# A hybrid decoder block on one core: score products issued in pairs on two row halves of TensorE, SSD products alternating between two column halves

## The chip, the core and the metric

The kernel runs on one core of a Trainium2 chip. Times are microseconds (us) of device time of one execution. The engines are TensorE (PE, with its weight loads listed as PEld), VectorE (DVE), ScalarE (ACT), GpSimd (POOL) and SyncE (SP), which issues most transfers. Each works through its own instructions in order.

## The reference, cut to what matters

One block over 1024 tokens of width 1024. Differential attention and a Mamba-2 SSD mixer read the same modulated input, are merged by gates, and a PEER layer follows that retrieves 128 experts a token. Two parts matter here.

```python
scores = jnp.einsum('bqhjd,bkhjd->bhjqk', q[:, q0:kend], k[:, :kend]).astype(jnp.float32) * scale
p = jax.nn.softmax(scores + bias[None, :, None], axis=-1)
a = p[:, :, 0] - lam * p[:, :, 1]
...
w = cb[..., None] * decay_ts * dtc[:, None]
y = jnp.einsum('btsgr,bsgrp->btgrp', w, xc)
y = y + jnp.einsum('btgn,bgrpn->btgrp', cc, state) * jnp.exp(cum)[..., None]
```

Each of the 8 attention heads has two score matrices (j = 0, 1), both with a contraction over 64 channels. Each of the 32 SSD heads gives 64 channels of y. Everything is in float32.

## The kernel before, in words

The tokens are worked in two halves of 512. A half goes through projections, attention, the SSD mixer, the merge, the first norm and the PEER scores; then the program does the same for the second half, and a dense PEER stage follows that goes through all experts for some token tiles. For the other tiles the experts' rows are gathered by indirect transfers on POOL ("side" work), and the top-16 routing on DVE is "urgent" work. A Python planner (`drive`, `step`) lays side and urgent steps between the steps of the main generator by costs written in the program (the numbers that are yielded). The order inside an engine is then set by the framework's scheduler, which follows priorities and its own simulated times. So an edit at one place can move instructions at others.

Most of TensorE's work is `projs` (L269): products of 128 rows by 128 columns with 512 moving columns, each split in three for precision. They have one record each in the trace. A float32 product (scores, SSD, transposes) has two records, so a count of 384 at L436 means 192 products.

Scores (`att_scores`, L420 to 457). A unit is one head and one tile of 128 queries; it has nk tiles of keys, 1 to 4 in the first half of the tokens and 5 to 8 in the second. `att_scores(u, j)` issues the products of one j: channels 64j to 64j+63, so they use one half of TensorE's rows (L436), in pieces of at most 512 keys, each into a PSUM bank of the tag "S", of which there are 3. DVE adds the bias, takes the minimum and frees the bank (L440). ScalarE takes the exponential (L445), and behind the second j DVE combines the two (L452 to 458). `attention` calls it for j = 0, lays in some projection work, and calls it for j = 1.

SSD (`ssd_head`, `ssd_pair`). `ssd_head` prepares a head's operands: it loads the running sums (`cr`), ScalarE makes the decays `w` and exponentials (L738 to 743), DVE multiplies them (L747, L752), and it returns a list `mm` of products: 5 a head in the first half (three of 256 columns, two of 128), 6 in the second (four and two). `ssd_pair` (L758) runs the lists of two heads into one bank: the first head's output takes partitions 0 to 63 and so uses columns 0 to 63 of TensorE, the second's the other 64 columns. All of the first list is issued, then all of the second. `ssd` calls it four times for each of four groups in each half of the tokens, 32 pairs in all, and prepares the next two heads behind each pair.

Of the kernel before, what the change touches and what calls it, by code (L numbers as in the profile page):

```python
# [11 lines left out]
F32 = mybir.dt.float32  # L12
# [4 lines left out]
AF = mybir.ActivationFunctionType  # L17
ALU = mybir.AluOpType
AX = mybir.AxisListType

P = 128
# [26 lines left out]
class Block:  # L48
# [370 lines left out]
        hd.ms = self.mp.tile([P, 4], F32, name="att_m", tag="att_m", bufs=2)  # L419
        return hd  # L420

    def att_scores(self, u, j):

        nc, hd = self.nc, u.hd
        n = u.nk * P
        off = 896 - (u.nk - 1) * P
        if j == 0:
            u.e, u.st = [], self.mp.tile([P, 10], F32, name="att_s", tag="att_s", bufs=6)
        e, st = self.four(f"e{j}"), u.st
        r = slice(j * 64, j * 64 + 64)  # L430

        low = 3.0e38
        for c0 in range(0, n, 512):
            w = min(512, n - c0)
            sc = self.psum("ps_s", tag="S")
            nc.tensor.matmul(  # L436
                sc[:, :w], hd.q[r, u.qt * P : u.qt * P + P], hd.ks[c0 // 512][r, :w], start=True, stop=True
            )
            at = 8 + j if c0 + w < n else j
            nc.vector.tensor_tensor_reduce(  # L440
                e[:, c0 : c0 + w], sc[:, :w], hd.bias[:, off + c0 : off + c0 + w], scale=-0.125,
                scalar=low, op0=ALU.add, op1=ALU.min, accum_out=st[:, at : at + 1],
            )
            low = st[:, at : at + 1]
        nc.scalar.activation(  # L445
            e[:, :n], e[:, :n], AF.Exp, scale=-1.0, bias=st[:, j : j + 1],
            accum_out=st[:, 2 + j : 3 + j],
        )
        u.e.append(e)
        if j:  # L450

            nc.vector.reciprocal(st[:, 4:6], st[:, 2:4])  # L452
            nc.vector.tensor_scalar(
                st[:, 6:7], st[:, 2:3], st[:, 5:6], self.neg_lam, op0=ALU.mult, op1=ALU.mult
            )
            nc.vector.scalar_tensor_tensor(
                u.e[0][:, :n], e[:, :n], st[:, 6:7], u.e[0][:, :n], op0=ALU.mult, op1=ALU.add
            )

    def att_turn(self, u):  # L460
# [38 lines left out]
    def attention(self, hb, hT, heads, big, start):  # L499

        fill, prev, done = iter(()), None, None

        def more(n=1):
            for x in islice(fill, n):
                yield x

        t = 0.43 + 0.4 * hb
        for i in range(4 * HEADS + 1):
            h, qt = divmod(i, 4)
            u = None  # L510
            if h < HEADS:
                if qt == 0:
                    while len(heads) <= h:
                        yield from more()
                    hd = self.head(hb, h, big[h], heads[h])
                u = SimpleNamespace(hd=hd, qt=qt, nk=hb * 4 + qt + 1)
            if u:
                self.att_scores(u, 0)
                yield t
            if qt != 0:  # L520
                yield from more()
            if u:
                self.att_scores(u, 1)
                yield t
            if prev:
                self.att_turn(prev)
                yield t
            if qt != 2:
                yield from more()
            if prev:  # L530
                self.att_values(prev)
                yield t
                if prev.qt == 3:
                    done = prev.hd
                    self.att_norm(done)
                elif prev.qt == 1 and done:
                    self.att_out(done)
            yield from more(99 if qt == 0 else 1)
            if qt == 0 and h + 1 == HEADS:
                fill = self.ssd_start(hb, hT, start)  # L540
            elif qt == 0 and h + 1 == len(heads):
                fill = self.qkv(hb, h + 1, hT, heads)
            prev = u
        self.last_head = done
# [213 lines left out]
    def ssd_pair(self, heads):  # L758

        yp = self.psum("ps_y", tag="S")  # L760
        for half, mm in enumerate(heads):
            for i, (o, n, l, r) in enumerate(mm):
                self.nc.tensor.matmul(  # L763
                    yp[half * 64 : half * 64 + 64, o : o + n], l, r, start=i == 0, stop=i == len(mm) - 1,
                    skip_group_check=True,
                )
        return yp
# [771 lines left out]
```

## Time and profile before

| | |
|---|---|
| time, median of 3 runs | 4873.54 us (4871.61 to 4889.75) |
| the profiled execution: its time | 4892.37 us |
| its span in the trace | 4890.7 us |
| TensorE busy | 4064.6 us (83%) |
| DVE busy | 2973.5 us (61%) |
| POOL busy | 1853.8 us (38%) |

The first half's SSD stage lies at about 440 to 920 us, the second half's attention at 1110 to 1500, its SSD stage at 1500 to 2230; the dense stage begins near 2670. A busy share is an average over the span; what bounds a stage is read from that stage. The start of a matmul's record is measured; its end is modelled, and the records of neighbours overlap, so the time that a product takes is read here from start to start.

### The profile page before, as it was taken

To read this page: it belongs to the slowest core of one execution; us is meant where nothing else is said; L and a number is where in the kernel's file an instruction comes from. 1 tells how busy PE (TensorE), PEld (TensorE's weight loads), DVE (VectorE), ACT (ScalarE), POOL (GpSimd) and SP (SyncE) were. 2 spreads that over 40 slices of the span, in tenths; PEclk is the share of its full clock that TensorE was granted. 3 is DMA by queue.
4 is the path that set the end of the run, shared out by engine and by line. 5 is a ranking of instruction groups with operands and counts; after the bars stand their busy time and mean duration, and the time that the engine had idled before them with its cause. 6 is when DMAs were issued, how large, how long until landed. Compare 5 with 4: busy or idle time off the path is not lost.

```text
span 4890.7 us, 52580 instructions
## 1 busy us (share of the span) xinstructions
PE 4064.6 (83%) x17996; PEld 2780.7 (57%) x17996; DVE 2973.5 (61%) x6965; ACT 1424.4 (29%) x2340; POOL 1853.8 (38%) x1720
## 2 busy tenths in 40 slices
PE   6999898998988999998765856867999888998155
PEld 4777676776656755556652425756656775556000
DVE  7664545558999853458973147999322884226920
ACT  3544444323343442432211112322222222222000
POOL 1000000000225743345385546454343674334774
PEclk7999999999898999999876975988999999999588
DMA  7323232443555866678688852998888998888998
GB/s 274 107 76 114 71 106 93 130 150 100 168 165 175 288 218 223 216 264 299 196 276 278 311 212 86 304 307 302 283 284 281 351 353 293 276 287 319 363 359 317
DMA packets 443648, 1134.14 MB, mean 232 GB/s; under 512 B 141852, under 2 KB 164532, under 8 KB 443380
## 3 DMA queue, kind: packets, MB, share of 16 engines
q0 software_dynamic: 191008, 676.42, 39.8%
q1 hardware_dynamic: 218804, 405.04, 25.5%
q10 hardware_dynamic: 33568, 49.32, 2.8%
q8 instruction: 143, 2.34, 0.2%
q14 instruction: 125, 1.02, 0.1%
HBM read 1066.51 MB, written 63.06 MB: 231 GB/s over the span
## 4 chain that ended last, share of the span: by engine, by line
PE 38%; DVE 15%; issue 12%; DMA 10%; POOL 7%; ACT 2%; SPq 1%; ACTq 0%; POOLq 0%; DVEq 0%
PE ps_y L1285 7%; PE ps_u L269 7%; PE ps_v L1325 6%; POOL grow L1177 5%; DVE grow L1120 4%; DMA grow<-in_peer_u,ei 3%; DMA grow<-in_peer_v,ej 3%; PE ps_x L269 3%; POOL second_k L1254 3%; PE ps_b L269 2%; DVE wlo L220 2%; PE ps_z L269 2%; PE ps_pq L269 2%; PE ps_y L763 2%; PE ps_g L269 2%
## 5 line engine op out<-in xcount | busy, mean ns | idle before, releaser
L1177 POOL DMA_INDIRECT grow<-in_peer_u,ei x640 | 848.1, 1325 | 970.1 <-DVE grow L1120 312.6
L1177 POOL DMA_INDIRECT grow<-in_peer_v,ej x640 | 669.5, 1046 | 804.9 <-PE ps_y L1285 668.6
L220 DVE TENSOR_TENSOR wlo<-wraw,whi 128x1024 fp32r<-128x1024 f32 x498 | 607.3, 1221 | 522.8 <-ACT whi L219 414.5
L219 ACT CAST whi<-wraw 128x1024 fp32r<-128x1024 f32 x498 | 519.9, 1047 | 1379.5 <-PE ps_u L269 523.7
L1120 DVE SCALAR_TENSOR_TENSOR grow<-grow,gh 128x1024 f32<-128x1024 f32 x640 | 771.6, 1221 | 93.9 <-DMA grow<-in_peer_u,ei 89.3
L1285 PE MATMUL ps_y<-grow,own 128*32 128x512 f32 x2560 | 609.9, 629 | 105.9 <-DMA grow<-in_peer_v,ej 76.8
L269 PE MATMUL ps_u<-hhi,whi 128*128 128x384 f32 x1024 | 363.9, 355 | 53.3 <-ACT whi L219 45.6
L269 PE MATMUL ps_u<-hhi,wlo 128*128 128x384 f32 x1024 | 364.2, 356 | 38.7 <-DVE wlo L220 38.7
L1254 POOL TENSOR_SCALAR second_k<-iota_c,at 128x128 f32<-128x128 f32 x384 | 301.1, 794 | 236.5 <-PE ps_gate L1285 183.8
L1147 DVE COPY own<-wt 128x4 f32<-128x4 f32 x160 | 29.7, 189 | 563.3 <-PE ps_y L1285 506.1
L978 POOL DMA_DIRECT2D h2s_d<-bighi x8 | 4.5, 561 | 936.3 <-ACT bighi L245 936.1
L269 PE MATMUL ps_u<-hlo,whi 128*128 128x384 f32 x1024 | 355.1, 347 | 0.0
L1285 PEld LDWEIGHTS ps_y<-grow,own 128*32 128x32 f32 x2560 | 90.1, 111 | 423.2 <-DMA grow<-in_peer_v,ej 205.1
L1285 PE MATMUL ps_gate<-first_k,second_k 128*128 128x128 f32 x768 | 195.7, 396 | 122.0 <-POOL second_k L1254 87.5
L1325 PE MATMUL ps_v<-wlo,ehi 128*128 128x512 f32 x768 | 257.2, 409 | 27.3 <-DVE wlo L220 27.0
L1325 PE MATMUL ps_v<-whi,ehi 128*128 128x512 f32 x768 | 226.6, 408 | 58.4 <-ACT whi L219 40.0
L269 PEld LDWEIGHTS ps_u<-hhi,whi 128*128 128x128 f32 x1024 | 201.2, 196 | 117.8 <-ACT whi L219 56.1
L269 PEld LDWEIGHTS ps_u<-hhi,wlo 128*128 128x128 f32 x1024 | 200.2, 196 | 98.2 <-DVE wlo L220 63.5
L1285 PEld LDWEIGHTS ps_gate<-first_k,second_k 128*128 128x128 f32 x768 | 155.5, 257 | 169.6 <-POOL second_k L1254 126.5
L1325 PE MATMUL ps_v<-whi,elo 128*128 128x512 f32 x768 | 251.2, 403 | 0.0
L1325 PEld LDWEIGHTS ps_v<-whi,ehi 128*128 128x128 f32 x768 | 142.4, 192 | 119.5 <-ACT whi L219 47.6
L269 PEld LDWEIGHTS ps_u<-hlo,whi 128*128 128x128 f32 x1024 | 200.7, 196 | 14.6 <-issue 10.9
(342 smaller groups left out, 8098.9 us busy)
## 6 DMA issues: line engine op xcount, KB each, us to landing
wraw<-in_w_in SPq DMA_DIRECT2D x160, 512.0 KB
wraw<-in_peer_uT SPq DMA_DIRECT2D x128, 512.0 KB
wraw<-in_peer_v SPq DMA_DIRECT2D x128, 512.0 KB
wada<-in_w_adaT SPq DMA_DIRECT2D x48, 512.0 KB
g_d<-gs ACTq DMA_DIRECT2D x48, 512.0 KB
gl<-g_d SPq DMA_DIRECT2D x48, 512.0 KB
cr<-cum_d SPq DMA_DIRECT2D x64, 256.0 KB
wraw<-in_w_ssd SPq DMA_DIRECT2D x32, 512.0 KB
```

Of the source, the lines that this page charges most:

```text
L219: nc.scalar.copy(hi, raw)
L220: i = nc.vector.tensor_tensor(lo, raw, hi.bitcast(F32), op=ALU.subtract)
L269: i = self.nc.tensor.matmul(ps, w[x][:, k, :], r[y][:, k, :], start=k + n == 0, stop=k == kk - 1 and n == 2)
L763: self.nc.tensor.matmul(yp[half * 64 : half * 64 + 64, o : o + n], l, r, start=i == 0, stop=i == len(mm) - 1, skip_group_check=True,)
L978: nc.gpsimd.dma_start(self.h2s_d[part][:, k, :], big[k][part][:, g0:])
L1120: nc.vector.scalar_tensor_tensor(u, u, 1.0, h2, op0=ALU.mult, op1=ALU.mult, accum_out=act[:, k : k + 1])
L1147: nc.vector.tensor_copy(own[:, :, OWN - 1].rearrange("p (h r) -> p h r", h=2), wt[:, b * n : b * n + n].rearrange("p (h r) -> p h r", h=2) ...
L1177: self.nc.gpsimd.indirect_dma_start(out=r, out_offset=None, in_=table, in_offset=bass.IndirectOffsetOnAxis(ap=ei[:, k : k + 1], axis=0),)
L1254: nc.gpsimd.tensor_scalar(second, self.iota_c, at[:, 1, k : k + 1], None, op0=ALU.is_equal)
L1285: return op(*args, **kw)
L1325: nc.tensor.matmul(acc[2 * tt + c], prev[x][:, tt * P : tt * P + P], v[y].rearrange("p k c -> p (k c)")[:, c * 512 : c * 512 + 512], start ...
```

## The change

`att_scores` is called once for each piece of 512 keys instead of once for each j. It takes two banks, issues the two products of the piece next to each other (row halves 0 and 1), then the two DVE reductions; with the last piece come the two exponentials and the combination. For units of at most 512 keys everything is in the first call, and the second step of `attention` issues nothing but still yields its cost. `ssd_pair` zips the two lists: product i of the first head, product i of the second, and so on. No product, transfer or DVE instruction is added or dropped.

```diff
--- before.py
+++ after.py
@@ -419,42 +419,45 @@
         hd.ms = self.mp.tile([P, 4], F32, name="att_m", tag="att_m", bufs=2)
         return hd
 
-    def att_scores(self, u, j):
+    def att_scores(self, u, c0):
 
         nc, hd = self.nc, u.hd
         n = u.nk * P
         off = 896 - (u.nk - 1) * P
-        if j == 0:
-            u.e, u.st = [], self.mp.tile([P, 10], F32, name="att_s", tag="att_s", bufs=6)
-        e, st = self.four(f"e{j}"), u.st
-        r = slice(j * 64, j * 64 + 64)
-
-        low = 3.0e38
-        for c0 in range(0, n, 512):
-            w = min(512, n - c0)
-            sc = self.psum("ps_s", tag="S")
+        if c0 == 0:
+            u.e, u.st = [self.four(f"e{j}") for j in range(2)], self.mp.tile([P, 10], F32, name="att_s", tag="att_s", bufs=6)
+            u.low = [3.0e38, 3.0e38]
+        st = u.st
+        w = min(512, n - c0)
+        scs = [self.psum("ps_s", tag="S") for _ in range(2)]
+
+        for j, sc in enumerate(scs):
+            r = slice(j * 64, j * 64 + 64)
             nc.tensor.matmul(
                 sc[:, :w], hd.q[r, u.qt * P : u.qt * P + P], hd.ks[c0 // 512][r, :w], start=True, stop=True
             )
-            at = 8 + j if c0 + w < n else j
+        last = c0 + w == n
+        for j, sc in enumerate(scs):
+
+            e, at = u.e[j], j if last else 8 + j
             nc.vector.tensor_tensor_reduce(
                 e[:, c0 : c0 + w], sc[:, :w], hd.bias[:, off + c0 : off + c0 + w], scale=-0.125,
-                scalar=low, op0=ALU.add, op1=ALU.min, accum_out=st[:, at : at + 1],
-            )
-            low = st[:, at : at + 1]
-        nc.scalar.activation(
-            e[:, :n], e[:, :n], AF.Exp, scale=-1.0, bias=st[:, j : j + 1],
-            accum_out=st[:, 2 + j : 3 + j],
-        )
-        u.e.append(e)
-        if j:
+                scalar=u.low[j], op0=ALU.add, op1=ALU.min, accum_out=st[:, at : at + 1],
+            )
+            u.low[j] = st[:, at : at + 1]
+            if last:
+                nc.scalar.activation(
+                    e[:, :n], e[:, :n], AF.Exp, scale=-1.0, bias=st[:, j : j + 1],
+                    accum_out=st[:, 2 + j : 3 + j],
+                )
+        if last:
 
             nc.vector.reciprocal(st[:, 4:6], st[:, 2:4])
             nc.vector.tensor_scalar(
                 st[:, 6:7], st[:, 2:3], st[:, 5:6], self.neg_lam, op0=ALU.mult, op1=ALU.mult
             )
             nc.vector.scalar_tensor_tensor(
-                u.e[0][:, :n], e[:, :n], st[:, 6:7], u.e[0][:, :n], op0=ALU.mult, op1=ALU.add
+                u.e[0][:, :n], u.e[1][:, :n], st[:, 6:7], u.e[0][:, :n], op0=ALU.mult, op1=ALU.add
             )
 
     def att_turn(self, u):
@@ -520,7 +523,8 @@
             if qt != 0:
                 yield from more()
             if u:
-                self.att_scores(u, 1)
+                if u.nk > 4:
+                    self.att_scores(u, 512)
                 yield t
             if prev:
                 self.att_turn(prev)
@@ -758,10 +762,11 @@
     def ssd_pair(self, heads):
 
         yp = self.psum("ps_y", tag="S")
-        for half, mm in enumerate(heads):
-            for i, (o, n, l, r) in enumerate(mm):
+
+        for i, pair in enumerate(zip(*heads)):
+            for half, (o, n, l, r) in enumerate(pair):
                 self.nc.tensor.matmul(
-                    yp[half * 64 : half * 64 + 64, o : o + n], l, r, start=i == 0, stop=i == len(mm) - 1,
+                    yp[half * 64 : half * 64 + 64, o : o + n], l, r, start=i == 0, stop=i == len(heads[0]) - 1,
                     skip_group_check=True,
                 )
         return yp
```

What the scheduler makes of it, on TensorE. First a pair in the second half's SSD stage (`ps_y_15562`; `w_15384` and `cr_15382` are the first head's operands, `w_15396` and `cr_15394` the second's; `ps_z` and `ps_x` are projections, `ps_gate` is routing work, `ps_y_13888` belongs to the gathers). Before:

```order
L269 MATMUL ps_z_15514<-hhi_6573,whi_15509 128x512
L763 MATMUL ps_y_15562<-w_15384,dtx_15014 64x128
L269 MATMUL ps_z_15514<-hlo_6574,whi_15509 128x512
L763 MATMUL ps_y_15562<-cr_15382,st0_15059 64x256
L269 MATMUL ps_z_15514<-hhi_6573,wlo_15510 128x512
L1285 MATMUL ps_y_13888<-grow_14117,own0_101 32x512 x2
L269 MATMUL ps_z_15514<-hhi_6573,whi_15509 128x512
L763 MATMUL ps_y_15562<-cr_15382,st1_15064 64x256
L269 MATMUL ps_z_15514<-hlo_6574,whi_15509 128x512
L763 MATMUL ps_y_15562<-w_15396,dtx_15013 64x256
L269 MATMUL ps_z_15514<-hhi_6573,wlo_15510 128x512
L763 MATMUL ps_y_15562<-w_15396,dtx_15013 64x128
```

After (the pair's first product stands some rows earlier):

```order
L768 MATMUL ps_y_15562<-w_15396,dtx_15013 64x256
L768 MATMUL ps_y_15562<-w_15384,dtx_15013 64x128
L768 MATMUL ps_y_15562<-w_15396,dtx_15013 64x128
L768 MATMUL ps_y_15562<-w_15384,dtx_15014 64x256
L1290 MATMUL ps_gate_14448<-first_k_14432,second_k_14433 128x128
L1290 MATMUL ps_gate_14448<-first_k_14437,second_k_14438 128x128
L1290 MATMUL ps_gate_14448<-first_k_14444,second_k_14445 128x128
L768 MATMUL ps_y_15562<-w_15396,dtx_15014 64x256
L768 MATMUL ps_y_15562<-w_15384,dtx_15014 64x128
L768 MATMUL ps_y_15562<-w_15396,dtx_15014 64x128
L768 MATMUL ps_y_15562<-cr_15382,st0_15059 64x256
L768 MATMUL ps_y_15562<-cr_15394,st0_15059 64x256
```

Before, nearly every product stood alone between projections, first one head's and then the other's; now they stand together and the heads alternate.

A pair in the first half's SSD stage (`w_4214`, `cr_4212` first head, `w_4226`, `cr_4224` second). Before:

```order
L763 MATMUL ps_y_4323<-w_4214,dtx_3965 64x256
L269 MATMUL ps_x_4374<-hlo_134,whi_4369 128x512
L763 MATMUL ps_y_4323<-w_4214,dtx_3965 64x128
L269 MATMUL ps_x_4374<-hhi_133,wlo_4370 128x512
L763 MATMUL ps_y_4323<-w_4214,dtx_3966 64x256
L269 MATMUL ps_x_4374<-hhi_133,whi_4369 128x512
L763 MATMUL ps_y_4323<-w_4214,dtx_3966 64x128
L269 MATMUL ps_x_4374<-hlo_134,whi_4369 128x512
L763 MATMUL ps_y_4323<-cr_4212,st1_4017 64x256
L269 MATMUL ps_x_4374<-hhi_133,wlo_4370 128x512
L763 MATMUL ps_y_4323<-w_4226,dtx_3965 64x256
```

After (the first head's first product stands 15 projection rows earlier):

```order
L269 MATMUL ps_x_4374<-hlo_134,whi_4369 128x512
L269 MATMUL ps_x_4374<-hhi_133,wlo_4370 128x512
L768 MATMUL ps_y_4323<-w_4226,dtx_3965 64x256
L768 MATMUL ps_y_4323<-w_4214,dtx_3965 64x128
L768 MATMUL ps_y_4323<-w_4226,dtx_3965 64x128
L768 MATMUL ps_y_4323<-w_4214,dtx_3966 64x256
L768 MATMUL ps_y_4323<-w_4226,dtx_3966 64x256
L269 MATMUL ps_x_4374<-hhi_133,whi_4369 128x512
L768 MATMUL ps_y_4323<-w_4214,dtx_3966 64x128
L269 MATMUL ps_x_4374<-hlo_134,whi_4369 128x512
L768 MATMUL ps_y_4323<-w_4226,dtx_3966 64x128
L269 MATMUL ps_x_4374<-hhi_133,wlo_4370 128x512
```

Here only part of the products stands together; others are still alone between projections.

Score products of the first half (`k_762`, `k_770` name the same head's keys). Before, `ps_s_1058` is j = 1 of one unit and `ps_s_1102` is j = 0 of the next:

```order
L476 MATMUL ps_av_944<-v_498,aT_916 128x128 x3
L467 MATMUL ps_aT_984<-ident_80,e0_891 128x128 x4
L436 MATMUL ps_s_1058<-k_762,q_761 128x256
L436 MATMUL ps_s_1102<-k_762,q_761 128x384
L269 MATMUL ps_k_1112<-hhi_133,wlo_1108 128x512
```

After, with `ps_s_1036` and `ps_s_1103` in the same roles:

```order
L479 MATMUL ps_av_944<-v_506,aT_916 128x128 x3
L470 MATMUL ps_aT_984<-ident_80,e0_890 128x128 x4
L436 MATMUL ps_s_1036<-k_770,q_769 128x256
L436 MATMUL ps_s_1103<-k_770,q_769 128x384
L269 MATMUL ps_k_1120<-hhi_133,whi_1115 128x512
```

The two rows stand as they did: the second product of a unit is beside the first of the next unit, on the other row half.

## Rows read from the trace of the kernel before

**Rows 1.** Busy time of each engine by stretch; the first row names the columns.
```profile
core 0: us, PE busy (x) PEld busy (x) DVE busy (x) ACT busy (x) POOL busy (x), PEclk, DMA share, GB/s
440.00:920.00 480.00, 441.46 (x1947) 328.35 (x1946) 265.11 (x474) 218.77 (x375) 0.00 (x0) 0.95 0.32 100
1110.00:1500.00 390.00, 348.81 (x1461) 234.26 (x1460) 371.90 (x1290) 162.18 (x341) 77.47 (x67) 0.89 0.46 141
1500.00:2230.00 730.00, 691.74 (x3140) 447.77 (x3139) 451.20 (x848) 278.45 (x452) 359.25 (x327) 0.96 0.71 238
2230.00:2670.00 440.00, 293.85 (x1278) 214.57 (x1276) 319.94 (x740) 81.78 (x94) 247.71 (x235) 0.80 0.79 258
```

**Rows 2.** Chain that ended last, from 1500 to 2230 us, shares by line.
```profile
by line: PE ps_x L269 16.0%; PE ps_y L1285 14.1%; PE ps_z L269 10.9%; PE ps_b L269 9.8%; PE ps_y L763 9.7%; issue 5.7%; DMA grow<-in_peer_u,ei 5.2%; PE ps_g L269 4.2%; POOL second_k L1254 3.3%; POOL grow L1177 2.7%; PE ps_gate L1285 2.1%; D
```

**Rows 3.** TensorE's waits, 440 to 920 us: total us, times, longest us.
```profile
PE ps_y L763 <- DVE w L747: 12.2, 3, 10.1
```

**Rows 4.** Groups of the SSD products: count, busy us, mean ns, idle before.
```profile
L763 PE MATMUL ps_y<-w,dtx 128*64 128x256 f32 x256 | 82.4, 407 | 12.5 <-DVE w L747 12.5
L763 PE MATMUL ps_y<-cr,st 128*64 128x256 f32 x192 | 55.9, 393 | 0.0
L763 PE MATMUL ps_y<-w,dtx 128*64 128x128 f32 x256 | 51.7, 284 | 0.0
```

**Rows 5.** Timeline of TensorE near 600 us: SSD products one at a time.
```profile
start us, us, engine line op out<-in xcount [idle before <-releaser]
599.59 0.49 PE L269 MATMUL ps_x<-hhi,wlo 128*128 128x512 f32 x1
600.01 0.43 PE L763 MATMUL ps_y<-w,dtx 128*64 128x128 f32 x2
600.38 0.49 PE L269 MATMUL ps_x<-hhi,whi 128*128 128x512 f32 x1
600.80 0.65 PE L763 MATMUL ps_y<-w,dtx 128*64 128x256 f32 x2
601.38 0.49 PE L269 MATMUL ps_x<-hlo,whi 128*128 128x512 f32 x1
601.80 0.43 PE L763 MATMUL ps_y<-w,dtx 128*64 128x128 f32 x2
602.16 0.50 PE L269 MATMUL ps_x<-hhi,wlo 128*128 128x512 f32 x1
602.74 0.39 PE L269 MATMUL ps_x<-hlo,whi 128*128 128x512 f32 x1
602.97 0.40 PE L269 MATMUL ps_x<-hhi,wlo 128*128 128x512 f32 x1
```

**Rows 6.** Timeline of TensorE near 1980 us, inside a longer run.
```profile
1979.54 0.38 PE L763 MATMUL ps_y<-cr,st 128*64 128x256 f32 x1
1979.54 0.43 PE L763 MATMUL ps_y<-w,dtx 128*64 128x256 f32 x1
1979.75 0.38 PE L763 MATMUL ps_y<-cr,st 128*64 128x256 f32 x1
1979.97 0.38 PE L763 MATMUL ps_y<-cr,st 128*64 128x256 f32 x1
```

**Rows 7.** Timeline of TensorE near 1974 us, rows 32 columns wide.
```profile
1974.35 2.78 PE L1285 MATMUL ps_y<-grow,own 128*32 128x512 f32 x24
```

**Rows 8.** Timeline of TensorE: two runs of score products.
```profile
1181.67 1.35 PE L436 MATMUL ps_s<-k,q 64*128 64x512 f32 x6
1223.19 1.98 PE L436 MATMUL ps_s<-k,q 64*128 64x512 f32 x4
```

**Rows 9.** What TensorE's idle time before the score products ended with (us, times).
```profile
  DVE att_s L440: 55.9, 58
```

**Rows 10.** Waits, 3030 to 3100 us: total us, times, longest us.
```profile
POOL grow L1177 <- DVE ei L1215: 53.0, 1, 53.0
```

## The prediction

> **What bounds the kernel now.** I read the table of stages first, because the change touches four of them and nothing else [rows 1]. TensorE is busy 441.5 of 480 us (92%) in the first half's SSD stage and 691.7 of 730 us (95%) in the second's, so there time taken from TensorE should come off the end. In the second half's attention DVE is busy 371.9 of 390 us and TensorE waits for it; score products that take less time change little there. Then the chain of waits in the second SSD stage [rows 2]: it runs through projections, gather products, and for 9.7% of its 730 us (71 us) through the SSD products at L763, with DMA grow at 5.2%. TensorE's waits in the first SSD stage come third: only 12.2 us for `w`, in 3 waits, the longest 10.1 [rows 3]. So the SSD products are limited by TensorE's own time, not by their operands. Last I read the timeline around single products, for prices.
>
> **Prices.** A product of 256 columns has two records, spaced 0.21 to 0.22 us in a run [rows 6], so 0.43 us; one of 128 half of that, 0.22. The program has 224 and 128 of these (half the record counts) [rows 4]: 224 x 0.43 + 128 x 0.22 = 124 us if nothing overlaps.
>
> A product that stands alone between projections costs more. From 599.59 to 602.16 us [rows 5] there are three projection products and SSD products of 128, 256 and 128 columns: 2.57 us. A projection product takes 0.23 (602.74 to 602.97), so the plain sum is 3 x 0.23 + 0.22 + 0.43 + 0.22 = 1.56, and three excursions to the 64-column form and back cost 1.01: 0.34 each.
>
> Do two products on different column halves overlap? [Rows 6] show the end of one head's list and the start of the other's side by side: records of `cr,st` start at 1979.54, 1979.75 and 1979.97, those of `w,dtx` at 1979.54 and 1979.81 between them. Each half keeps its 0.22 and neither slows the other. With four strips of 32 columns, 24 gather records of 512 columns take 2.78 us [rows 7], 0.12 each, where a 512-column record alone would take twice 0.22. So the overlap is real for these float32 products. Rows overlap too: a run of six records of score products on both row halves takes 1.35 us, and another of four, all on one half, 1.98 [rows 8].
>
> **The change part by part.** (1) SSD pairs. I walked TensorE's order before and after with these prices: a product starts when the one before it has started and its own half is free, and any other instruction ends a run. In the first half that gives 51.4 us before and 38.9 after, in 65 and 61 runs; in the second 66.1 and 42.6, in 70 and 43 runs. The first half gains less because its products still stand alone in many places (second place of the order shown). Gain in TensorE time: first half 12.5 + 4 x 0.34 = 13.9 us; second half 23.5 + 27 x 0.34 = 32.7 us. Of that I take the share that TensorE is busy in these stages, 0.92 and 0.95: 12.8 + 31.0 = 43.8 us.
>
> (2) Scores. By the order only 26 of the 96 pairs of a head stand next to each other after the change (8 before). A pair needs two of the three S banks, which DVE frees one at a time, and TensorE already waited 55.9 us for that in 58 places [rows 9]. What stands between is other work. And before the change products of different units met on different row halves, in 47 places; after it there are 64. The same walk gives 28.9 to 27.9 us in the first half, with 46 runs in both, and 75.2 to 68.5 in the second, with 3 runs more. The first is worth 1 us. The second, 6.7 - 1.0 = 5.7 us, lies under DVE's 371.9 of 390 us: I take 0. If DVE gave way all of it would come, which bounds it.
>
> (3) Waits that are added. Each product of the first head is now queued behind one of the second, so a pair ends its first list only when the second head's `w` is there. Behind it stand the projections of the next heads, and ScalarE and DVE wait for those. No row shows this wait; the nearest is 12.2 us for three [rows 3]. Below, it is -12.2 (these three go away, since the scheduler now puts the products later); above, see the second rival. I take 3 us, near the row's smaller waits, as ScalarE and DVE are busy only 219 and 265 of the 480 us. The exponentials of both j now come together behind the last piece; the transposes that read them belong to the next unit, so I take 0 for that, with the other work of the unit as cover.
>
> (4) What is late next. The gathers are paced by the program's order, not by time, and move along with TensorE. DMA is at 0.71 in the second SSD stage [rows 1]; with 31 us less it would be 0.74. The dense stage and the tail only start earlier.
>
> Sum: 43.8 + 1 - 3 = 42 us. On the profiled execution, 4892.4 us (4890.7 of span and 1.7 around it), this gives 4850. The median of the runs shown is 4873.5, and 42 of 4892 of that is 42: **4831.5 us**.
>
> **Rivals.** *The second SSD stage gives nothing back*, because gathers and routing (POOL 359 of 730 us, DMA 0.71) take the place of TensorE's time. For it: `issue` and DMA grow have 10.9% of that chain [rows 2]. Against: TensorE's 95%. Then only the first half's 12.8 + 1 stays, 4860 us.
>
> *Slower: the second head's `w` is late in the first pair of each group.* Its two heads are prepared right before, from a load of `cr` through ScalarE and DVE, and TensorE's queue now stops at the second product. At the longest wait seen, 10.1 us [rows 3], in all 8 groups: 81 - 42 = +39, 4912 us. It decides from 42 / 8 = 5.3 us a group. Against it: the order puts projection rows between a pair's first product and the rest, which is the scheduler's room for that wait.
>
> *The change doesn't do what it says: column halves don't overlap when they alternate.* Only the 31 excursions saved would stay, 31 x 0.34 = 10.5 us, with the TensorE share 10, and less the 3 of waits 7: 4867 us. In favour, each alternate product needs weights of its own on the same rows; against, [rows 6 and 7]. The Trainium skill would take this side: TensorE: Matmul & The Clock Gate, Part 3 (Packing small matmuls), says that weight loads overlap running products only when the row group differs, which is not so here. The trace speaks against it, with starts 0.22 apart in each half.
>
> *The scheduler's order elsewhere.* It moved on all engines, also in the dense stage, where the change has no edit. One wait there is 53.0 us of POOL for routing [rows 10]; half of it either way is 26 us: 4806 or 4858.
>
> **How the numbers follow.** About 0.5%, 24 us, is what a measurement can tell from no change here. Chances: forecast 0.60 (its own range 4815 to 4850), nothing from the second stage 0.15, slower 0.08, no overlap 0.06, order elsewhere 0.06 for the gain and 0.05 for the loss. Faster by over 0.5% is under 4849: nearly all of the forecast and the gain, 0.64. Slower by over 0.5% is over 4898: 0.08. The rest, 0.28, is the same. The range leaves out the slower rival and a little at each end: 4803 to 4868.
>
> **What would show it.** In the profile after, the `ps_y` products of the SSD take about 13 us less in the first SSD stage and some 30 less in the second, with records of the two `w` 0.22 us apart in each half and in pairs; the stages end that much sooner; scores in the second half's attention change and its length does not. Wrong would be: TensorE waiting for DVE `w` at `ps_y` for over 20 us in a stage; the stages shorter and the gathers' wait behind them longer by the same; or the dense stage, 2670 to the end, over 15 us longer or shorter, which would be the order elsewhere.

## The result, and the profile after

The median of the kernel after is 4814.08 us (4799.33 to 4822.5) against 4873.54: 59.5 us less, a ratio of 0.9857 (95% interval 0.9835 to 0.988). A second measurement beside the experiments gave 0.9868 (0.9846 to 0.9891). The forecast was 42 us less, 4831.5.

The stages of the kernel after, to set beside [rows 1] (columns as there):

```profile
440.00:920.00 480.00, 444.12 (x2032) 334.84 (x2031) 277.69 (x501) 230.59 (x395) 0.00 (x0) 0.95 0.34 106
1110.00:1500.00 390.00, 344.76 (x1455) 231.35 (x1454) 381.48 (x1296) 167.67 (x352) 80.58 (x68) 0.88 0.43 140
1500.00:2230.00 730.00, 668.15 (x3139) 437.30 (x3138) 474.55 (x923) 278.08 (x447) 391.49 (x358) 0.94 0.76 258
2230.00:2670.00 440.00, 316.19 (x1432) 230.12 (x1430) 289.33 (x655) 86.14 (x102) 242.91 (x226) 0.83 0.78 254
```

The stretches are the same, the work in them is not: more of what follows has moved into them. In the second half's attention DVE is still full (381.5 of 390 us).

The groups of the SSD products, as in [rows 4]:

```profile
L768 PE MATMUL ps_y<-w,dtx 128*64 128x256 f32 x256 | 68.4, 416 | 19.4 <-DVE w L751 19.3
L768 PE MATMUL ps_y<-cr,st 128*64 128x256 f32 x192 | 46.7, 405 | 0.0
L768 PE MATMUL ps_y<-w,dtx 128*64 128x128 f32 x256 | 49.9, 297 | 0.0
```

The counts are those of before; busy time fell from 190.0 to 165.0 us. These busy times leave out overlap but hold modelled ends. From start to start, with waits left out, the products of the first half occupy some 50.6 us of TensorE in the trace (65.3 before), those of the second 51.1 (74.4). TensorE's wait for DVE `w` rose from 12.5 to 19.3 us. A pair of the second half that stands together, in the timeline:

```profile
1660.74 1.52 PE L768 MATMUL ps_y<-w,dtx 128*64 128x256 f32 x16
1662.10 1.03 PE L768 MATMUL ps_y<-cr,st 128*64 128x256 f32 x8
```

All 24 records of a pair (12 products) run from 1660.74 to 1663.13, 2.39 us (this end is modelled); one after the other they would take 8 x 0.43 + 4 x 0.22 = 4.3 by the prediction's prices. That is what [rows 6] promised.

The chain from 1500 to 2230 us, as in [rows 2]:

```profile
by line: PE ps_y L1290 14.6%; PE ps_x L269 14.4%; PE ps_z L269 11.0%; DMA grow<-in_peer_u,ei 9.9%; PE ps_b L269 8.3%; issue 6.8%; POOL grow L1182 5.3%; PE ps_y L768 5.0%; POOL second_k L1259 4.0%; DVE grow L1125 2.8%; PE ps_g L269 2.8%; PE 
```

The SSD products fell from 9.7% to 5.0%, and waits for gathered rows of `peer_u` rose from 5.2 to 9.9%.

Now the stages by their own bounds, from the first to the last SSD product of the first half, and the tail behind the last dense product. Before:

```profile
447.20:833.00 385.80, 353.32 (x1571) 256.95 (x1570) 214.36 (x393) 187.19 (x334) 0.00 (x0) 0.95 0.28 90
4540.90:4890.70 349.80, 133.96 (x514) 19.75 (x513) 142.27 (x285) 2.91 (x6) 223.40 (x212) 0.76 0.93 347
```

After:

```profile
451.70:812.70 361.00, 336.83 (x1579) 248.25 (x1578) 214.11 (x394) 186.97 (x334) 0.00 (x0) 0.96 0.31 96
4492.70:4820.70 328.00, 134.99 (x513) 19.66 (x513) 141.19 (x285) 2.92 (x6) 217.77 (x211) 0.76 0.96 370
```

The first SSD stage is 24.8 us shorter: 16.5 of it busy time, the rest idle time. It ends 20.3 us earlier than before, as it starts 4.5 later. The tail has the same work and is 22 us shorter, at 370 GB/s in place of 347; more on that below.

Three marks tell how the gain goes on: the load of `gy` (the first gathered tile is done), the first product `ps_u` of the dense stage on the main path, and its first `ps_v`, which needs the routing of the last tiles. In each row the first of the two times behind the comma is the one to read (first and last start). Before:

```profile
L1171 SPq DMA_DIRECT2D gy<-y_d x5: 320/326/327, 2162.5 to 4871.5; - x5
L269 PE MATMUL ps_u<-hhi,whi x1024: 331/334/689, 2500.4 to 4463.1; 128*128 128x384 f32 x171
L1325 PE MATMUL ps_v<-whi,ehi x768: 387/393/796, 3057.3 to 4537.8; 128*128 128x512 f32 x192
```

After:

```profile
L1176 SPq DMA_DIRECT2D gy<-y_d x5: 319/326/327, 2097.8 to 4801.6; - x5
L269 PE MATMUL ps_u<-hhi,whi x1024: 331/334/689, 2504.5 to 4416.3; 128*128 128x384 f32 x171
L1330 PE MATMUL ps_v<-whi,ehi x768: 387/393/796, 3009.3 to 4489.6; 128*128 128x512 f32 x192
```

The gathered tile is done 64.7 us earlier, the main path reaches the dense stage 4.1 us later, and the second part of that stage starts 48.0 us earlier. From there to the last `ps_v` product the distance stays at 48. So the gain of the second SSD stage does not come out where I looked for it.

The place where it comes out lies between the last two marks. Behind its first 24 `ps_u` products TensorE takes routing and gather products of another tile, and the 25th `ps_u` product follows them: at 2661.83 us before, at 2611.76 after. These 50 us are there before `ps_v` starts; from the 25th product to `ps_v` both kernels need about 396 us. TensorE's wait for POOL's routing between the 24th and the 25th product, and the 25th, before (2507 to 2662 us):

```profile
PE ps_gate L1285 <- POOL second_k L1254: 57.8, 19, 4.7
2661.83 0.44 PE L269 MATMUL ps_u<-hhi,whi 128*128 128x384 f32 x1
```

After (2510 to 2612 us):

```profile
PE ps_gate L1290 <- POOL second_k L1259: 12.3, 5, 5.6
2611.76 0.69 PE L269 MATMUL ps_u<-hhi,whi 128*128 128x384 f32 x1
```

The prediction named a dense stage over 15 us longer or shorter as the sign of the order elsewhere, and this sign came: from the first `ps_v` to the end the kernel after needs 22 us less (1811.4 for 1833.4), all of it in the tail.

### The profile page after: what moved, and what is told of

Same layout as the page of the kernel before. It is cut to its first block, busy times and chain, and to the rows that moved or that the text cites. A ratio compares the mean times of both kernels' runs of the same rounds, so it can differ in the third digit from the quotient of the medians.

```text
span 4820.7 us, 52596 instructions
## 1 busy us (share of the span) xinstructions
PE 4016.2 (83%) x17996; PEld 2752.8 (57%) x17996; DVE 2974.3 (62%) x6965; ACT 1423.7 (30%) x2340; POOL 1881.6 (39%) x1720
## 4 chain that ended last, share of the span: by engine, by line
PE 54%; DVE 18%; DMA 13%; issue 8%; POOL 5%; ACT 2%; SPq 1%; DVEq 0%; ACTq 0%; POOLq 0%
PE ps_u L269 9%; PE ps_v L1330 8%; PE ps_y L1290 7%; DVE grow L1125 5%; PE ps_x L269 5%; DMA grow<-in_peer_v,ej 5%; PE ps_b L269 4%; DMA grow<-in_peer_u,ei 3%; PE ps_z L269 3%; PE ps_g L269 2%; POOL grow L1182 2%; DVE wlo L220 2%; POOL second_k L1259 2%; PE ps_vT L269 2%; PE ps_pq L269 2%
## 5 line engine op out<-in xcount | busy, mean ns | idle before, releaser
L1182 POOL DMA_INDIRECT grow<-in_peer_v,ej x640 | 681.8, 1065 | 731.1 <-PE ps_y L1290 589.0
```

Source lines behind the costliest of these rows:

```text
L1182: self.nc.gpsimd.indirect_dma_start(out=r, out_offset=None, in_=table, in_offset=bass.IndirectOffsetOnAxis(ap=ei[:, k : k + 1], axis=0),)
```

## The experiments

"Walk" is the prediction's: time of the SSD products in the two halves by the order, each with its number of runs. The last three columns are the marks, from one trace each.

| kernel | walk, first and second half, us (runs) | median less its before, us | ratio and 95% interval | `gy` | first `ps_u` | first `ps_v` |
|---|---|---|---|---|---|---|
| before | 51.4 (65), 66.1 (70) | | | 2162.5 | 2500.4 | 3057.3 |
| after | 38.9 (61), 42.6 (43) | -59.5 | 0.9857 (0.9835 to 0.988) | 2097.8 | 2504.5 | 3009.3 |
| SSD only | 39.3 (62), 41.7 (38) | -47.5 | 0.9896 (0.9876 to 0.9916) | 2129.9 | 2520.5 | 3025.8 |
| scores only | 51.2 (61), 65.2 (53) | -12.9 | 0.9974 (0.9961 to 0.9988) | 2156.9 | 2556.4 | 3056.9 |
| no overlap | 55.3 (58), 69.1 (45) | -1.2 | 0.9996 (0.9983 to 1.001) | 2131.7 | 2560.5 | 3058.2 |
| swapped | 49.7 (57), 62.2 (31) | -31.6 | 0.9938 (0.9921 to 0.9954) | 2134.9 | 2524.9 | 3022.5 |
| first half | 38.9 (61), 65.2 (53) | -40.0 | 0.9913 (0.9897 to 0.9929) | 2126.5 | 2531.0 | 3027.8 |
| second half | 51.2 (61), 42.6 (43) | -36.9 | 0.9923 (0.9904 to 0.9942) | 2125.6 | 2520.2 | 3015.4 |
| chained | 28.3 (17), 40.4 (40) | -48.1 | 0.9899 (0.9883 to 0.9916) | 2079.4 | 2579.1 | 3011.5 |
| second first | 32.6 (43), 36.1 (32) | -55.0 | 0.9885 (0.9868 to 0.9902) | 2126.6 | 2522.4 | 3024.6 |
| more main work | 38.9 (61), 42.6 (43) | -48.0 | 0.9897 (0.988 to 0.9915) | 2105.3 | 2550.9 | 3020.6 |

**The SSD pairs alone.** The kernel before with the second hunk of the change.

> The alternating SSD pairs alone; scores as before. Theory A (TensorE's time in the two SSD stages is what is saved: products that overlap plus excursions to the 64-column form at 0.34 us): by the walk of its order 39.3 us in 62 runs and 41.7 us in 38, so 46 us less than before, all of the change's gain. Theory B (the scheduler's new order elsewhere made the 17 us that the forecast lacks): a time anywhere from 20 to 75 us less. Theory C (the scores give a part): some 15 us behind the whole change.

47.5 us less. The SSD pairs make most of the change's gain. The number is theory A's, but it lies in theory B's range as well, and it is 12 us behind the whole change where theory C has 15; the runs below part them.

**The scores alone.** The kernel after with the old `ssd_pair`.

> The scores alone in pieces; SSD pairs as before. Theory A: the score products take 1 us less where TensorE is the limit, but the scheduler's new order also gives the SSD products 61 and 53 runs in place of 65 and 70: 9 us less in all, within 0.5% of before. Theory C: 15 us or more less, with the second half's attention shorter. If DVE's limit there is worse for the new order: slower, attention over 370 us.

12.9 us less, and in a second measurement 0.9983 (0.9971 to 0.9994), 9.7 us; small, but there. It is near the 9 of theory A, but the marks don't show it where theory A has it.

```profile
L1175 SPq DMA_DIRECT2D gy<-y_d x5: 319/326/327, 2156.9 to 4848.6; - x5
L269 PE MATMUL ps_u<-hhi,whi x1024: 331/335/690, 2556.4 to 4460.2; 128*128 128x384 f32 x171
L1329 PE MATMUL ps_v<-whi,ehi x768: 386/394/797, 3056.9 to 4533.1; 128*128 128x512 f32 x192
```

`ps_v` starts 0.4 us earlier than before, although the main path is 56 us late; in the second trace it starts 5.3 us later than before. The expectation of that second run:

> The scores alone a second time: 0.9974 of before again (0.9961 to 0.9988) if those 12 us are the kernel's; 0.999 or more if they came with the runs. No stage in its first trace shows them: its dense stage's second part starts 0.4 us from where the kernel before starts it.

The second ratio lies inside the interval that was expected, and the stage that makes it was not found.

**No overlap.** Both heads write columns 0 to 63:

```diff
+        self.nc.vector.memset(yp[64:128, :], 0.0)
-                    yp[half * 64 : half * 64 + 64, o : o + n], l, r, start=i == 0, stop=i == len(heads[0]) - 1,
+                    yp[0:64, o : o + n], l, r, start=i + half == 0, stop=half == 1 and i == len(heads[0]) - 1,
```

> The whole change, but both heads of a pair write the same 64 columns of TensorE, so that the alternating order stays and nothing can overlap; the second head's y is left out (zeros), and DVE gets 32 small memsets. Theory A: 55.3 us in 58 runs and 69.1 in 45: 5 us less than before, so 40 behind the change. If the order and not the overlap gives the gain: 40 us or more less than before.

The gain is gone with the overlap, though the order still alternates. The memsets add DVE work (222.0 us busy in the first SSD stage, 214.1 without), so the 1.2 us are not an exact price of the order alone. This kernel's gathered tile is done 30.8 us earlier than before, and its `ps_v` starts 0.9 us later: an earlier gathered tile by itself brought nothing here.

**The second head first, without alternating.** The kernel before with its loop turned round:

```diff
-        for half, mm in enumerate(heads):
+        for half, mm in reversed(list(enumerate(heads))):
```

> The kernel before with one thing changed: of a pair the second head's products are all issued first, then the first head's. Nothing overlaps by design; the scheduler makes another order, with 57 and 31 runs in place of 65 and 70. Theory A: 49.7 us and 62.2 us, so 20 us less than before, almost all of it from 47 fewer excursions. If excursions cost nothing on the path: no change. Theory B: the scatter of such a reorder, up to 25 us either way.

31.6 us less, with nothing that overlaps by design. 47 runs fewer at 0.34 us are 16 us, and the walk 5.6. So excursions are on the path; that each costs more than its price isn't shown, since theory B's scatter is larger than the 10 us that are left over. Half of what the change brings can be had here by issuing the second head first, which is prepared last.

**One half of the tokens alone.** `ssd_pair` alternates only where `hb` is 0, or only where it is 1 (cut to the lines that set the order).

```diff
+        n = len(heads[0])
+        order = [(i, half) for i in range(n) for half in range(2)]
+        if hb != 0:
+            order = [(i, half) for half in range(2) for i in range(n)]
```

> The whole change, but the pairs alternate in the first half's SSD stage alone. Theory A: by the walk 38.9 us in 61 runs there and 65.2 in 53 in the second half: 12.8 + 6.4 + 1 = 20 us less than before; the first SSD stage as short as with the whole change (361 us in place of 386). A rival, that the first half's gain is lost again before the end: 9 us less, as with the scores alone.

> The whole change, but the pairs alternate in the second half's SSD stage alone. Theory A: 51.2 us in 61 runs and 42.6 in 43: 1.5 + 31 + 1 = 33 us less than before. The rival of the forecast (the second stage gives nothing back at the end): 9 us less.

40.0 and 36.9 us less. Together with the scores counted once (40.0 + 36.9 - 12.9 = 64.0) they give about the whole change. The second stage does give something back at the end, so that rival falls. Both kernels hold the change of the scores, so they are best set beside the scores alone: the first half is then worth about 27 us and the second about 24. The first half's 27 stand in the trace as they are: its SSD stage ends at 810.0 us there and at 837.1 with the scores alone.

**Runs that may not be broken.** In `ssd_pair`, for each product `m` (cut):

```diff
+                self.behind(m.ins, self.last)
+                self.last = m.ins.name
```

> The whole change, and each product of a pair is ordered behind the one before it and behind the last projection product, the next projection behind the pair: 28.3 us in 17 runs and 40.4 in 40. Theory A: 36 + 34 + 1 = 71 us less than before, 27 less than the whole change by the same sum. Rival: a pair that may not be broken waits for the late head's operand with nothing to fill it: TensorE waits over 25 us for DVE w and the time is that of the whole change or more.

The rival held: 48.1 us less, no better than the change. The first SSD stage and its first wait:

```profile
446.00:806.40 360.40, 316.00 (x1533) 242.12 (x1533) 217.90 (x398) 185.00 (x332) 0.00 (x0) 0.90 0.30 92
```

```profile
PE ps_y L768 <- DVE w L751: 28.4, 9, 9.8
```

With 44 runs fewer the stage lasts 360.4 us against 361.0: waits for `w` are 28.4 us (13.0 in the kernel after), the wait of `ps_bt` for DVE `held`, which the change had lost, is back with 9.4, and the granted clock is 0.90 (0.96).

**The second head first, alternating.** `reversed(list(enumerate(pair)))` in the change's inner loop.

> The whole change, and of each two alternating products the second head's goes first. Its operands come last, so the scheduler has no reason to let one product go ahead alone: 32.6 us in 43 runs and 36.1 in 32 (the whole change: 38.9 in 61 and 42.6 in 43). Theory A: 12.4 x 0.92 + 10.2 x 0.95 = 21 us less than the whole change, some 80 less than before. Rival, as with the chained pairs: longer runs are given back as waits for DVE w (over 20 us in the first SSD stage) and a lower clock, and the time is that of the whole change or more.

55.0 us less, not 80: theory A ends here. The products occupy another 17 us less of TensorE than with the change (84.3 against 101.6) and nothing comes of it. The rival's time held, its sign only in part: waits for `w` in the first SSD stage are 16.7 us (13.0 with the change) and not over 20, and in the second 2.2 (6.3). The first stage has 34.5 us of idle time in place of 24.2, a granted clock of 0.93 in place of 0.96, and lasts 367.1 us in place of 361.0. Its longest wait, in the timeline and then in stretches before, in and behind it:

```profile
555.51 2.83 PE L768 MATMUL ps_y<-w,dtx 128*64 128x256 f32 x16 [11.63 <-DVE w L751]
```

```profile
530.00:543.00 13.00, 13.00 (x49) 9.64 (x49) 2.97 (x4) 3.66 (x5) 0.00 (x0) 0.93 0.13 40
543.50:555.50 12.00, 0.38 (x1) 0.00 (x0) 2.83 (x7) 6.89 (x17) 0.00 (x0) 0.73 0.57 154
555.50:559.00 3.50, 3.49 (x20) 2.10 (x20) 2.03 (x5) 1.70 (x4) 0.00 (x0) 0.50 0.02 5
564.00:570.00 6.00, 6.00 (x29) 3.26 (x27) 3.75 (x7) 4.80 (x9) 0.00 (x0) 1.00 0.19 44
```

TensorE waits 11.63 us for DVE `w`; the granted clock is 0.73 in that stretch and 0.50 (1.2 GHz) in the next, which is the run of products, and full (2.4 GHz) in the last row. So a part of what the longer runs save is paid with this wait, and the clock adds to it; where the rest goes was not found.

**More work on the main path.** Each second query product of the second half is computed twice (cut):

```diff
+            if hb and hj % 2:
+                self.projs(ws, hT, ps)
```

> The whole change, and 8 of the second half's 16 PEER query products are computed twice (the second overwrites the first): 8 x 24 x 0.227 = 44 us more of TensorE's work on the main path just before the dense stage. Theory G (there the gathers' chain decides and the main path has room): the first dense product comes some 40 us later, the dense stage's second part (ps_v) starts within 15 us of where it did, and the time is within 15 us of the whole change. Rival (the main path decides): the time grows by 40 us or more.

```profile
L1179 SPq DMA_DIRECT2D gy<-y_d x5: 320/326/327, 2105.3 to 4813.6; - x5
L269 PE MATMUL ps_u<-hhi,whi x1024: 331/334/689, 2550.9 to 4424.3; 128*128 128x384 f32 x171
L1333 PE MATMUL ps_v<-whi,ehi x768: 387/395/796, 3020.6 to 4497.5; 128*128 128x512 f32 x192
```

The added work is smaller than the expectation says: the trace has 168 `ps_pq` products more, 7 query products of 24 (the step `hj` = 1 has none of its own), so 38 us and not 44. The first `ps_u` comes 46.4 us later than with the change, the first `ps_v` 11.3, and the ratio is 0.9897 against 0.9857 and 0.9868: 14 to 20 us. Three quarters of the delay at `ps_u` are absorbed before `ps_v`, and the rival's 40 us do not appear, so theory G holds in the main; its bound of 15 us for the time is kept by one of the two comparisons and missed by the other, so the main path's room has an end. The chained kernel shows the same without being made for it: its main path is 78.7 us later than before, and `ps_v` starts 45.8 us earlier.

**The two kernels of the first measurement again.**

> The whole change again, beside the others: 0.986 of before, as measured (0.9835 to 0.988).

> The kernel before a second time, for its trace. If the first trace's tail (from the last dense product to the end, 350 us, where nine other traces have 328 to 333) was one slow execution, it is 328 to 335 here, and the start of the dense stage's second part lies at 3057 us within 8. If the tail belongs to the kernel, it is 345 or more again, and 15 us of the change's gain are made there.

The kernel after gave 0.9868, its `ps_v` started at 3004.0. The kernel before gave 1.0006 (0.9994 to 1.0018), `ps_v` at 3057.3 and a tail of 351.8 us. By my own rule the tail would then belong to the kernel; but the scores alone had 331.6 in their first trace and 346.4 in the one taken beside this. The tail differs by 15 us between executions of one kernel. All ten traces of kernels whose SSD pairs were changed have 328 to 333, both of the kernel before about 350; I leave open whether the change shortens it.

## Why the prediction was right, and where it was off

- **The prices** were right. Two column halves overlap in full (2.39 us for a pair), and without it the gain is gone. The Trainium skill's rule that weight loads overlap only with a running product of another row group (TensorE: Matmul & The Clock Gate, Part 3) does not hold for these pairs: both heads use all 128 rows. One reading was loose: of the six score records in [rows 8] two have only 128 columns, so 1.35 us is not the time of six full ones.
- **The first SSD stage** was under-sized: 12.8 us forecast, 20.3 earlier at its end. The run with the first half alone makes it 27 us at the end. I multiplied the product time by TensorE's busy share, as if the idle time scaled. It moved by itself. TensorE's wait for the end of a group (`ps_bt` behind DVE `held`, 9.4 us in three before) is gone after. That part comes with the order that the scheduler happened to make, and the forecast had no term for it, so it is luck: the SSD change alone has nearly the same walk, and its stage is 374.8 us long, 2.6 us of it that wait:

```profile
448.70:823.50 374.80, 344.94 (x1579) 253.50 (x1578) 214.43 (x394) 187.99 (x334) 0.00 (x0) 0.94 0.30 92
```

- **The second SSD stage**: 31 us forecast; 24 by the run with the second half alone, and 28 is what the start of `ps_v` gains beyond the first stage (48 - 20). But the forecast had that stage's end moving, and the last SSD product is only 29 us earlier (8.7 beyond the first stage). This step failed in its place: the size was near, the way was another. Part (4) of the prediction let the gathers move along with TensorE; they moved further. Up to the first gathered tile POOL waits 39 us less for TensorE's gather products, before (1677.6 to 2171.2 us) and after (1660.7 to 2108 us):

```profile
POOL grow L1177 <- PE ps_y L1285: 183.6, 86, 11.4
POOL grow L1182 <- PE ps_y L1290: 144.6, 82, 10.4
```

That TensorE's freed time does this is not shown: without overlap the wait is 149.7 us. The main path lost its lead between the last SSD product and the first `ps_u`, 327.7 us before and 360.8 after. The largest waits of TensorE there, before (2172 to 2500 us) and after (2144 to 2504 us), the second for a routing product:

```profile
PE ps_hT L950 <- ACT v L938: 19.2, 2, 18.8
PE ps_key L1290 <- DVE ln1t L238: 31.5, 1, 31.5
```

The scores alone have the second one too (31.4), so it belongs to the scheduler's order and not to the overlap. Then the chains meet at the 25th `ps_u` product, where TensorE waits for POOL's routing 45.5 us less than before (57.8 and 12.3), and from there every kernel needs between 392 and 401 us to its first `ps_v`. So in these kernels the routing and the gathers decide when the dense stage goes on, and the main path has some room. Which step of the routing is the deciding one was not tested.

- **The scores**: 1 us forecast, about 10 measured (12.9 and 9.7). It is the term that is furthest off by its factor. Its order has 21 runs fewer of SSD products than before, worth 7 us at 0.34, but no run shows that this is the cause; it is open.
- **The added waits**: 3 us forecast, 7 measured (12.5 to 19.3). The slower rival, 10 us a group, did not come with the change; it came, in smaller form, with the chained pairs (28.4 us in the first SSD stage, 20.8 in the second).
- **The sum**: 42 forecast; 48 and 53 by the start of `ps_v` in the two traces, about 60 in the medians. The rest lies behind the dense stage or in the scatter of the tail. The number came out in the range because the overlap and the excursions were priced rightly; that most of what was sized too small or had no term (the scores, the idle time, the order) fell to the good side was luck.

## What to carry to other kernels

Products on one half of TensorE's columns were worth pairing with the other half here, and worth keeping together: a product alone between full ones cost 0.34 us more. For row halves the rows show the overlap, but no stage here showed a gain from it. When two lists alternate, nearly every product of the first waits behind one of the second, so the later operand holds up both; read from the order how long the runs get, and stop where TensorE begins to wait for operands. A stage that gets shorter need not end the program sooner: look at which chain decides at the next point where chains meet, before asking how much earlier the stage ends.

## What the runs showed that I had not expected

Turning round two heads' order, with no instruction more or less, was worth 0.9938 (0.9921 to 0.9954). In one wait of 11.6 us the granted clock fell, and the 3.5 us behind it, which are the run that had been waited for, went at 0.50. Without overlap the first gathered tile was still done 30.8 us earlier, and nothing came of it.
